# Embedding gather plus position add: streams and semaphores written by hand, and chunks of two sequences instead of one

## The chip, the cores and the metric

The kernel runs on one core of one Trainium2 chip. The metric is device microseconds of that core; lower is better. The kernel before has a median of 184.83 us over 4 runs (184.72 to 184.98).

## The reference

For each of 32 sequences of 512 indices a row of 512 float32 numbers (2 KB) is taken out of a table of 50000 rows, and the row of the position is added. Nothing is reused but the position rows, so 32 MiB (33.55 MB) are read from the table and 32 MiB are written.

```python
def reference(indices, embedding_table, position_embed):
    # indices (32, 512), table (50000, 512) f32, position_embed (512, 512) f32
    token_embed = embedding_table[indices]
    return (token_embed + position_embed).astype(np.float32)
```

## The kernel before

A sequence b is laid out over 128 partitions with K = 4 consecutive positions in each, so partition p holds positions 4p to 4p+3. The position rows are loaded once (line 56, four DMAs of 256 KB), copied by ScalarE to PSUM (line 79, `pos_ps0` to `pos_ps3`), and stay there. The indices come twice: those of sequence 0 straight into the layout that a gather wants (`idx0`, line 49), and all of them in rows (`idx_raw`, line 51), which VectorE turns to float (line 68), TensorE transposes (line 73) and VectorE turns back to int32 (`idx_t`, line 75).

Then the loop over b runs. For each k of 0 to 3 GpSimd (POOL) issues one indirect DMA (line 88) that gathers 128 rows of 2 KB, 256 KB in all, into `data[:, j, :]`; VectorE (DVE) adds `pos_ps[k]` in place (line 94); and after the n parts of a chunk SyncE (SP) issues the store (line 97). A chunk is a whole sequence for most b: one store of 1 MB in which each partition writes 4 rows that lie together, 8 KB. The first two sequences and the last one are cut into four stores of 256 KB with 2 KB for each partition, the four after the start and the last but one into two of 512 KB with 4 KB. There are 128 gathers, 128 adds and 46 stores.

The order is not written out by hand: the tile framework orders the instructions, gives each DMA one of eight semaphores for gathers and one of eight for plain transfers, and inserts the waits. So a gather waits for the gather eight before it, a store for the store eight before it, and a gather into a used buffer (a pool of 20 buffers of 8 KB for each partition) for that buffer's store as well. A wait that doesn't fit onto an instruction is an instruction of its own ahead of it on the same engine. At the end SP waits for all these semaphores, two for each waiting instruction, before the engines meet in a closing barrier. Each engine works through its instructions in order. Gathers and stores go through different queues to the same 16 DMA engines.

Of the kernel before, what the change touches and what calls it, by code (L numbers as in the profile page):

```python
# [1 line left out]

# [4 lines left out]

P = 128
K = 4
BUFS = 20  # L10


@with_exitstack
def kernel(
    ctx: ExitStack,
    tc: tile.TileContext,
    indices: bass.AP,
    embedding_table: bass.AP,
    position_embed: bass.AP,
    out: bass.AP,  # L20
):

    nc = tc.nc
    f32 = mybir.dt.float32
    i32 = mybir.dt.int32
    add = mybir.AluOpType.add

    B, S = indices.shape
    V, D = embedding_table.shape
    assert S == P * K and B == 32  # L30
    assert V < (1 << 24), "an index passes through float32"


    idx_words = indices.bitcast(i32)
    idx_first = idx_words[0].rearrange("(p w) -> p w", p=P)
    out_rows = out.rearrange("b (p k) d -> b p k d", k=K)
    pos_rows = position_embed.rearrange("(p k) d -> p k d", k=K)
    table = embedding_table[:, :]

    const = ctx.enter_context(tc.tile_pool(name="const", bufs=1))  # L40
    data_pool = ctx.enter_context(tc.tile_pool(name="data", bufs=BUFS))
    psum = ctx.enter_context(
        tc.tile_pool(name="psum", bufs=1, space=bass.MemoryType.PSUM)
    )

    idx0 = const.tile([P, 2 * K], i32)
    nc.sync.dma_start(out=idx0[:], in_=idx_first)
    idx_raw = const.tile([B, S, 2], i32)  # L50
    nc.sync.dma_start(
        out=idx_raw[:], in_=idx_words.rearrange("b (s w) -> b s w", w=2)
    )
    pos_sb = [const.tile([P, D], f32, name=f"pos_sb{k}") for k in range(K)]
    for k in range(K):
        nc.sync.dma_start(out=pos_sb[k][:], in_=pos_rows[:, k, :])


    ones = const.tile([B, B], f32)
    nc.gpsimd.memset(ones[:], 1.0)  # L60
    ident = const.tile([B, B], f32)
    nc.gpsimd.affine_select(  # L62
        out=ident[:], in_=ones[:], pattern=[[-1, B]],
        compare_op=mybir.AluOpType.is_equal, fill=0.0, base=0,
        channel_multiplier=1,
    )
    idx_f = const.tile([B, P, K], f32)
    nc.vector.tensor_copy(  # L68
        out=idx_f[:].rearrange("b p k -> b (p k)"), in_=idx_raw[:, :, 0]
    )  # L70
    turned = psum.tile([P, K, B], f32)
    for k in range(K):
        nc.tensor.transpose(turned[:, k, :], idx_f[:, :, k], ident[:])  # L73
    idx_t = const.tile([P, K, B], i32)
    nc.vector.tensor_copy(out=idx_t[:], in_=turned[:])  # L75

    pos_ps = [psum.tile([P, D], f32, name=f"pos_ps{k}") for k in range(K)]
    for k in range(K):
        nc.scalar.copy(out=pos_ps[k][:], in_=pos_sb[k][:])  # L79

    def chunk(b, parts):
        at = 0
        for n in parts:
            data = data_pool.tile([P, n, D], f32, tag="data")
            for j in range(n):
                k = at + j
                where = idx0[:, 2 * k : 2 * k + 1] if b == 0 else idx_t[:, k, b : b + 1]
                nc.gpsimd.indirect_dma_start(  # L88
                    out=data[:, j, :],
                    out_offset=None,  # L90
                    in_=table,
                    in_offset=bass.IndirectOffsetOnAxis(ap=where, axis=0),
                )
                nc.vector.tensor_tensor(  # L94
                    out=data[:, j, :], in0=data[:, j, :], in1=pos_ps[k][:], op=add
                )
            nc.sync.dma_start(out=out_rows[b][:, at : at + n, :], in_=data[:])  # L97
            at += n

    for b in range(B):  # L100
        if b <= 1 or b == B - 1:
            chunk(b, (1, 1, 1, 1))
        elif b <= 5 or b == B - 2:
            chunk(b, (2, 2))
        else:
            chunk(b, (K,))


# [1 line left out]
_INS = ['indices', 'embedding_table', 'position_embed']  # L110
_OUTS = [((32, 512, 512), 'float32')]


# [23 lines left out]
```

## Time and profile before

| what | value |
|---|---|
| median of 4 runs | 184.83 us |
| the profiled execution's own time | 184.92 us |
| span from its first to its last instruction | 183.2 us, so 1.7 us lie around it |
| POOL, 128 gathers of about 0.945 us | 121 us busy, from 2.8 to 163.4 us |
| DVE, 128 adds of 0.687 us | 87 us busy |
| ACT, PE | 3.6 us and 0.7 us busy, all at the start |
| moved by DMA | 68.33 MB, 373 GB/s over the span |

The busy time of POOL is the time in which it makes the descriptors of a gather, not the transfer; the transfers are in the DMA rows. In the rows by slices each digit or number is one fortieth of the span, 4.58 us. A store or load shows on SP (as SPq) only with the time of its issue.

### The profile page before, as it was taken

To read this page: it belongs to the slowest core of one execution; us is meant where nothing else is said; L and a number is where in the kernel's file an instruction comes from. 1 tells how busy PE (TensorE), PEld (TensorE's weight loads), DVE (VectorE), ACT (ScalarE), POOL (GpSimd) and SP (SyncE) were. 2 spreads that over 40 slices of the span, in tenths; PEclk is the share of its full clock that TensorE was granted. 3 is DMA by queue.
4 is the path that set the end of the run, shared out by engine and by line. 5 is a ranking of instruction groups with operands and counts; after the bars stand their busy time and mean duration, and the time that the engine had idled before them with its cause. 6 is when DMAs were issued, how large, how long until landed. Compare 5 with 4: busy or idle time off the path is not lost.

```text
span 183.2 us, 480 instructions
## 1 busy us (share of the span) xinstructions
PE 0.7 (0%) x4; PEld 0.6 (0%) x4; DVE 87.7 (48%) x130; ACT 3.6 (2%) x5; POOL 121.7 (66%) x134
## 2 busy tenths in 40 slices
PE   0000000000000000000000000000000000000000
PEld 0000000000000000000000000000000000000000
DVE  1253553645545444555555464454547464644400
ACT  2500000000000000000000000000000000000000
POOL 4777777777777777777777777777877677750000
DMA  4989999999999999999999999999999999999900
GB/s 133 311 285 361 364 382 380 396 391 409 402 399 388 425 404 405 400 411 419 422 411 413 418 414 413 412 412 418 415 420 412 416 411 424 406 424 409 369 12 0
DMA packets 17635, 68.33 MB, mean 373 GB/s; under 512 B 3008, under 2 KB 3008, under 8 KB 14560
## 3 DMA queue, kind: packets, MB, share of 16 engines
q0 software_dynamic: 10240, 33.56, 48.2%
q1 hardware_dynamic: 7392, 34.74, 46.3%
q14 instruction: 3, 0.02, 0.0%
HBM read 34.74 MB, written 33.55 MB: 373 GB/s over the span
## 4 chain that ended last, share of the span: by engine, by line
issue 43%; DMA 27%; POOL 14%; SPq 5%; POOLq 3%; DVE 1%
DMA data<-in_embedding_table_dram,idx_t 20%; POOL data L88 14%; DMA out_dram<-data 6%; SPq L97 5%; POOLq L88 3%; DVE data L94 1%; DMA idx<-in_indices_dram 1%
## 5 line engine op out<-in xcount | busy, mean ns | idle before, releaser
L88 POOL DMA_INDIRECT data<-in_embedding_table_dram,idx_t x124 | 117.2, 945 | 38.6 <-issue 37.4
L94 DVE TENSOR_TENSOR data<-data,pos_ps 128x512 f32<-128x512 f32 x128 | 86.8, 687 | 80.5 <-issue 54.0
L88 POOL DMA_INDIRECT data<-in_embedding_table_dram,idx x4 | 4.0, 993 | 2.5 <-DMA idx<-in_indices_dram 1.6
L79 ACT COPY pos_ps<-pos_sb 128x512 f32<-128x512 f32 x4 | 2.4, 589 | 4.5 <-DMA pos_sb<-in_position_embed_dram 3.7
L68 DVE CAST idx_f<-idx_raw 32x512 f32<-32x512 int32 x1 | 0.6, 639 | 3.5 <-DMA idx_raw<-in_indices_dram 3.5
L79 ACT ACT_TABLE_LOAD x1 | 1.3, 1283 | 0.8 <-PEq L121 0.8
L75 DVE CAST idx_t<-turned 128x128 int32<-128x128 f32 x1 | 0.3, 291 | 0.8 <-PE turned L73 0.8
L73 PE MATMUL turned<-ident,idx_f 32*128 32x32 f32 x4 | 0.7, 300 | 4.3 <-DVE idx_f L68 4.3
L73 PEld LDWEIGHTS turned<-ident,idx_f 32*128 32x128 f32 x4 | 0.6, 206 | 4.3 <-issue 4.3
L121 POOL MEMSET const-float32-0.0<- 128x1 f32 x1 | 0.1, 104 | 0.3 <-issue 0.3
L60 POOL MEMSET ones<- 32x32 f32 x1 | 0.1, 114 | 0.3 <-POOLq L121 0.3
L62 POOL TENSOR_SCALAR_AFFINE_SELECT ident<-ones 32x32 f32<-32x32 f32 x1 | 0.2, 203 | 0.1
L121 POOL MEMSET const-uint8-127<- 128x1 uint8 x1 | 0.1, 121 | 0.0
L121 POOL MEMSET const-bfloat16-1.0<- 128x1 bf16 x1 | 0.1, 115 | 0.0
L121 POOL MEMSET const-float32-1.0<- 128x1 f32 x1 | 0.1, 107 | 0.0
## 6 DMA issues: line engine op xcount, KB each, us to landing
out_dram<-data SPq DMA_DIRECT2D x24, 1024.0 KB
out_dram<-data SPq DMA_DIRECT2D x10, 512.0 KB
out_dram<-data SPq DMA_DIRECT2D x12, 256.0 KB
data<-in_embedding_table_dram,idx_t POOLq DMA_INDIRECT x124
pos_sb<-in_position_embed_dram SPq DMA_DIRECT2D x4, 256.0 KB
idx_raw<-in_indices_dram SPq DMA_DIRECT2D x1, 128.0 KB
data<-in_embedding_table_dram,idx POOLq DMA_INDIRECT x4
idx<-in_indices_dram SPq DMA_DIRECT2D x1, 4.0 KB
```

The lines of the kernel that those rows point to most:

```text
L60: nc.gpsimd.memset(ones[:], 1.0)
L62: nc.gpsimd.affine_select(out=ident[:], in_=ones[:], pattern=[[-1, B]], compare_op=mybir.AluOpType.is_equal, fill=0.0, base=0, channel_mul ...
L68: nc.vector.tensor_copy(out=idx_f[:].rearrange("b p k -> b (p k)"), in_=idx_raw[:, :, 0])
L73: nc.tensor.transpose(turned[:, k, :], idx_f[:, :, k], ident[:])
L75: nc.vector.tensor_copy(out=idx_t[:], in_=turned[:])
L79: nc.scalar.copy(out=pos_ps[k][:], in_=pos_sb[k][:])
L88: nc.gpsimd.indirect_dma_start(out=data[:, j, :], out_offset=None, in_=table, in_offset=bass.IndirectOffsetOnAxis(ap=where, axis=0),)
L94: nc.vector.tensor_tensor(out=data[:, j, :], in0=data[:, j, :], in1=pos_ps[k][:], op=add)
L97: nc.sync.dma_start(out=out_rows[b][:, at : at + n, :], in_=data[:])
L121: nc = _bacc.Bacc("TRN2", target_bir_lowering=False, num_devices=1)
```

## The change

Everything after the tiles are made is put into one critical section, within which the framework orders nothing and sets no waits: five streams of instructions, one for each engine, with semaphores by hand. Each gather, add and store carries its waits itself. Sixteen semaphores take turns for the gathers, so a gather waits for the one sixteen before it; a store's semaphore is waited for only where its slot is used again, and the last ones share one semaphore, on which SP waits once at the end.

The chunk becomes two sequences: K = 8, so each partition holds 8 consecutive positions, 16 KB; partitions 0 to 63 belong to the first sequence of the pair and 64 to 127 to the second. There are 16 units of 8 gathers of 256 KB, 11 slots of 16 KB for each partition, and 22 stores: most of them are 2 MB with 16 KB for each partition; unit 0 is stored in parts of 2, 2 and 4 gathers, unit 1 in 4 and 4, the last unit in 4, 2, 1 and 1.

As both halves of the partitions need the same position rows, the table of positions is loaded once (four DMAs of 256 KB, two issued by SP and two by ScalarE) and copied twice into PSUM: 16 copies of 64 partitions instead of 4 of 128. It fills all of PSUM, so the transposed indices are put in the last eighth of it, and the copies of the last position wait until they have been read. There are 8 small transposes instead of 4. The load of all indices moves from second to last on SP's queue, behind the position loads that SP issues.

```diff
-K = 4
-BUFS = 20
+K = 8
+H = P // 2
+SLOTS = 11
+LANES = 16
...
+    stores = []
+    for u in range(U):
+        parts = {0: (2, 2, 4), 1: (4, 4), U - 1: (4, 2, 1, 1)}.get(u, (K,))
...
+    def load_pos(engine, k):
+        half, at = divmod(k, K // 2)
+        engine.dma_start(
+            out=pos_sb[half * H : (half + 1) * H, at : at + 2, :],
+            in_=pos_rows[:, k : k + 2, :],
+        ).then_inc(s_pos[k // 2], 16)
+
+    with tc.tile_critical(no_gpsimd_drain=True):
+
+
+        nc.sync.dma_start(out=idx0[:], in_=idx_first).then_inc(s_first, 16)
+        load_pos(nc.sync, 0)
+        load_pos(nc.scalar, 4)
+        load_pos(nc.sync, 2)
+        load_pos(nc.scalar, 6)
+        nc.sync.dma_start(
+            out=idx_raw[:], in_=idx_words.rearrange("u (s w) -> u s w", w=2)
+        ).then_inc(s_raw, 16)
...
+        nc.gpsimd.wait_ge(s_first, 16)
+        for g in range(U * K):
+            u, k = divmod(g, K)
+            if g == K:
+                nc.gpsimd.wait_ge(s_idx, 1)
+            if u >= SLOTS and k == 0:
+                done = sum(1 for x in stores if x[0] == u - SLOTS)
+                nc.gpsimd.wait_ge(s_out[u - SLOTS], 16 * done)
+            where = idx0[:, 2 * k : 2 * k + 1] if u == 0 else idx_t[:, k, u : u + 1]
+            ins = nc.gpsimd.indirect_dma_start(
+                out=slots[u % SLOTS][:, k, :],
...
+            ).then_inc(s_gather[g % LANES], 16)
+            if g >= LANES:
+                ins._wait_ge(s_gather[g % LANES], rounds(g - LANES))
...
+        for g in range(U * K):
+            u, k = divmod(g, K)
+            if u == 0:
+                nc.vector.wait_ge(s_ps, 2 * (k + 1))
+            part = slots[u % SLOTS][:, k, :]
+            nc.vector.tensor_tensor(
+                out=part, in0=part, in1=pos_ps[:, k, :], op=add
+            )._wait_ge(s_gather[g % LANES], rounds(g)).then_inc(s_add, 1)
+
+
+        for k in range(K):
+            half, at = divmod(k, K // 2)
+            if k % 2 == 0:
+                nc.scalar.wait_ge(s_pos[k // 2], 16)
+            if k == K - 1:
+                nc.scalar.wait_ge(s_idx, 1)
+            for to in range(2):
+                nc.scalar.copy(
...
+        for u, at, n in stores:
+            done = s_out.get(u, s_rest)
+            rest += done is s_rest
+            nc.sync.dma_start(
+                out=out_rows[u][:, at : at + n, :],
+                in_=slots[u % SLOTS][:, at : at + n, :],
+            )._wait_ge(s_add, u * K + at + n).then_inc(done, 16)
+        nc.sync.wait_ge(s_rest, 16 * rest)
```

## The prediction

> **What bounds the kernel now.** I read the page's slices first, then groups, waits, stretches, last the end of the timeline.
>
> ```profile
> POOL 4777777777777777777777777777877677750000
> DMA  4989999999999999999999999999999999999900
> ...
> q0 software_dynamic: 10240, 33.56, 48.2%
> q1 hardware_dynamic: 7392, 34.74, 46.3%
> ...
> L88 POOL DMA_INDIRECT data<-in_embedding_table_dram,idx_t x124 | 117.2, 945 | 38.6 <-issue 37.4
> L94 DVE TENSOR_TENSOR data<-data,pos_ps 128x512 f32<-128x512 f32 x128 | 86.8, 687 | 80.5 <-issue 54.0
> ```
>
> DMA is full from the second slice to the 38th, and 48.2 + 46.3% of 183.2 us is 173 us of transfer on every engine. POOL looks only 7 tenths busy, but its idle time is "issue": between two gathers lie 0.30 us that nothing releases. It works at its own pace, 0.945 + 0.30 = 1.25 us a gather.
>
> ```profile
> POOL data L88 <- issue: 38.3, 123, 0.7
> ...
> POOL data L88 <- DMA data<-in_embedding_table_dram,idx_t: 1.2, 4, 0.3
> ```
>
> In the whole run it waits 1.2 us for transfers. From 2.81 to 163.45 us it issues 128 gathers: a floor.
>
> ```profile
> 10.00:20.00 10.00, 0.00 (x0) 0.00 (x0) 4.75 (x7) 0.00 (x0) 7.56 (x9) 1.00 0.97 324
> 20.00:40.00 20.00, 0.00 (x0) 0.00 (x0) 10.17 (x15) 0.00 (x0) 15.12 (x17) 1.00 1.03 391
> ...
> 120.00:140.00 20.00, 0.00 (x0) 0.00 (x0) 10.76 (x17) 0.00 (x0) 14.94 (x17) 1.00 1.02 415
> ...
> 175.00:184.00 9.00, 0.00 (x0) 0.00 (x0) 0.00 (x0) 0.00 (x0) 0.00 (x0) 1.00 0.00 0
> ```
>
> The last two columns are DMA share and GB/s. A gather (0.262 MB) and its store each 1.25 us want 419 GB/s; DMA gives 415. So two limits lie within 1% of each other. And in the last 9 us nothing runs at all.
>
> ```profile
> 171.84 3.51 SPq L97 DMA_DIRECT2D out_dram<-data  x2
> 171.90 0.69 DVE L94 TENSOR_TENSOR data<-data,pos_ps 128x512 f32<-128x512 f32 x1 [0.54 <-DMA out_dram<-data]
> ```
>
> The page doesn't count semaphore instructions; the trace's records have them. The last store packet ends at 174.6. SP then goes through ten instructions that wait for semaphores, at 176.04, 177.43, 178.15, 178.84, 179.54, 180.24, 180.94, 181.65, 182.34 and 182.34: most are 0.70 apart, though the same kind took 0.017 in mid-run. From 182.34 the closing barrier takes 0.85.
>
> **What the Trainium skill says.** "DMA: Bandwidth & Descriptors", section "Queues, rings and completion order": each engine goes round between the queues that have work, one packet at a time. The trace agrees: an engine has 8 packets of a 1 MB store, 8 x (311 + 163.5 ns, below) = 3.8 us if one gather packet stands between each two, and the store issued at 160.76 ran from 163.74 to 167.79, 4.05. Same page, "Why small descriptors are slow": each packet carries a fixed cost. Packet records, median ns for one engine:
>
> ```
> 2 KB store 84 (1536 of them)   4 KB store 159   8 KB store 309 (mean 311)
> 4 KB gather 159, mean 163.5 from 60 us on; 214 beside 2 KB stores (10 to 20 us)
> semaphore write 9
> ```
>
> That is 9 ns and 75 for every 2 KB. "Perfetto Trace Analysis", "Identifying Dependency Chains": waits that don't fit stand as instructions ahead; SP's list here shows one before nearly every store.
>
> **The change, part by part.** My sum follows the end: last gather, its add, its store, SP's closing.
>
> *Entry.* A hand-over from SP to all engines, one semaphore each way: barrier instructions in this trace are 0.04 to 0.1 us apart; I take 0.2 (0.1 to 0.5). It moves POOL's first gather, so everything.
>
> *Positions, indices.* 12 more ACT copies are 12 x 0.589 = 7.1 us, 4 more transposes about 0.5, a cast twice as long 0.6. Two loads issued from ACT (about 0.43 each, as on SP) push its table load (1.28) to 3.1 us, still before the first position rows at 4.73. Position k is then ready at 4.7 + 1.2(k+1), the last at 14.3. `idx_raw` goes behind two position loads on SP's queue and shares with ACT's two: 1 MB took until about 8 us before, so I let it land at 7.3 instead of 3.5. Cast 1.2, transposes 1.2, cast 0.3: `idx_t` at 10.0. POOL needs it for gather 8 at 3.0 + 8 x 1.25 = 13.0, so 3 us of cover. If that is gone, all 120 remaining gathers stand behind this wait and each us of lateness is a us at the end. The first add, behind both casts on DVE, moves from 8.2 to about 10. Taken: 0.
>
> *Semaphores in the middle.* The lanes of eight cost POOL 1.2 us at most; sixteen allow a lag of 20 us, so this can go. The five slot waits look at stores issued some 90 us earlier: 0. The instructions taken from DVE and SP were off the path there. Range -1.2 to 0, taken: 0, since a POOL that is earlier meets full DMA.
>
> *Packets of 16 KB.* By the line above 9 + 8 x 75 = 609 ns (an estimate; not seen here; if it is cut in two, 618). Per engine and pair of sequences: before 32 gather packets x 163.5 + 16 store packets x 311 + 10 x 9 = 5.23 + 4.98 + 0.09 = 10.30 us; the stretches show 1.02 for full, so 10.10 of wall against POOL's 10.00. After: 5.23 + 8 x 609 = 4.87, + 0.08 = 10.18, or 9.98. DMA goes from 1% too slow to just even. What it lost has been a growing lag: from end of issue to add, 4.5 to 6.8 us around 45 us, 6.7 to 8.5 near the end, so 2 us. Gain at most 2.
>
> *Stores twice as large.* A 2 MB store stands on the engines for 8 x (609 + 163.5) = 6.2 us. In that time 5 gathers, 20 packets for each engine, arrive and 8 are served; 12 x 0.16 = 2 us of lag are added at its end. I follow the end of the run with a base lag of 4 us: gather 119 is issued by 153.6, its add done at 158.3, the store starts 2.7 later (as the 8 KB stores do) and runs from 161 to 167.2. Gathers 124 to 127 wait behind it, share the engines with the 1 MB part until 171, and the last lands at 171.5. So the gain of 2 is given back: last add 171.9 to 172.6 and last store packet at 174.6, as before. With 0.2 of entry, 174.8. From both sides: 172 where the lag at the end stays near 5 us, 179 where gather packets take 170 ns beside 16 KB ones (the rival below).
>
> *Fewer stores early.* Unit 2's store leaves at about 37.5, where before there was one every 2 us. Between 27.5 and 37.5 the engines have 1 MB of stores (2.5) and 8 gathers (5.1), so 2.4 us idle. They cost nothing while POOL sets the pace; they count if DMA does.
>
> *Closing.* After the last packet, 0.4 to the semaphore. Then one wait for `s_rest` and about seven instructions on SP, four with waits, instead of ten waits: if as fast as mid-run 0.3, at 0.70 each 4.9. Both slow stretches of SP in this trace (36.9 to 40.2 and from 170.4) come after the small-packet stores; the change has half as many 2 KB packets at the end and no waiting instructions between the stores. That speaks for the fast side without showing it; I take 1.3. Barrier 0.85.
>
> Sum: 174.8 + 0.4 + 1.3 + 0.85 = 177.35 of span, against 183.2. Around it lie 184.92 - 183.2 = 1.7: 179.0 us. The profiled execution is 0.09 above the median, which I leave.
>
> **Rivals.** *The closing stays slow.* SP's 0.70 for each instruction is not tied to their number. Then 4.9 instead of 1.3, up to the old 7.7: 182.6 to 185. For it: it began before the final waits, on ordinary stores.
>
> *DMA gets better than even.* Gathers beside small stores took 214 and 187 ns early; that disappears, the lag at the end is 5 us: last add at 168.7, last packet about 171, and a fast closing: 171.2 + 0.4 + 0.3 + 0.85 + 1.7 = 174.5; with my 1.3, 175.5. Against it: the last 2 MB store.
>
> *Slower: large packets starve the gathers.* Place: 16 KB store packets beside gathers from unit 2 on. If a gather packet takes 170 ns or more beside them instead of 163.5, a pair needs 10.4 us, 0.4 over POOL's pace, and 13 such units lose 5 us: last packet at 179.8. With a closing of 0.4 + 1.3 + 0.85 that is 184.1, with the slow one (4.9) 187.7. It decides from about 170 ns with a slow closing, 171 with mine. For it: early gathers beside stores at 174 to 187 ns. Against it: the packets got faster, not slower, as the stores grew (163.5 beside 8 KB).
>
> That the change doesn't do what it says is excluded: the built program has the 16 KB stores and one wait on SP at its end.
>
> **How the numbers follow.** Likeliest (last packet 174 to 175.5, short closing, 177.5 to 181): 0.50. Slow closing: 0.20, 0.04 of it within 0.2% of before and 0.01 slower. Better DMA: 0.17. Slower: 0.13, 0.01 of it at no change. Faster by over 0.2% (what a measurement here can tell) 0.82, same 0.05, slower 0.13. Range 175.5 to 184.6: left out are about 0.05 below and 0.14 above.
>
> **What would show it.** Right: no row of waits on SP after the last store; POOL at 1.25 us a gather; stretches from 40 us at about 419 GB/s; last add near 172. Packets of 16 KB near 609 ns and gathers at 160 to 165 settle the fourth part. Wrong: a gap on POOL before gather 8, lags over 9 us, gather packets over 170 ns, or SP still at 0.70 for each instruction after the last packet.

## The result, and the profile after

The kernel after takes 185.02 us (median of 32 runs, 184.56 to 185.3), the kernel before beside it 184.78 (52 runs, 184.6 to 185.12). The ratio is 1.0012, interval 1.0007 to 1.0017: 0.24 us slower, where 5.8 us faster was forecast. The profiled execution of after took 184.94 us with a span of 183.2, that of before 184.92 with 183.2. In two of the five groups of experiments the kernel before itself takes 178.2 to 178.5 us instead of 184.5, because a stretch of slow waits at the end of SP, described below, is missing there; so each ratio belongs to the runs of its own group.

The page of after: slices, DMA queues, groups.

```profile
POOL 3777777777777777777777777777777778750000
DMA  5999999999999999999999999999999999999960
...
q0 software_dynamic: 10240, 33.56, 49.2%
q1 hardware_dynamic: 3504, 34.22, 45.5%
q10 hardware_dynamic: 160, 0.52, 1.1%
...
L128 POOL DMA_INDIRECT slot<-in_embedding_table_dram,idx_t x120 | 113.5, 946 | 36.6 <-issue 36.6
L157 DVE TENSOR_TENSOR slot<-slot,pos_ps 128x512 f32<-128x512 f32 x128 | 85.8, 687 | 77.8 <-DMA slot<-in_embedding_table_dram,idx_t 51.5
```

POOL is as before: 946 ns a gather, and idle time that is only "issue". DMA is not: its row goes on into the 39th slice, where before it ended with the 38th. The packets of stores and loads fell from 7392 to 3664 (q10 has the loads that ScalarE issues), but their share of the engines did not fall with them: 46.6% for 46.3%. The share of the gathers rose from 48.2 to 49.2%. And DVE, whose idle time was mostly "issue" before, now waits for gathers.

The waits of after (total, times, longest, in us):

```profile
DVE slot L157 <- DMA slot<-in_embedding_table_dram,idx_t: 51.5, 25, 4.3
POOL slot L128 <- issue: 38.7, 127, 0.3
...
DVE idx_f L146 <- DMA idx_raw<-in_indices_dram: 9.1, 1, 9.1
...
POOL slot L128 <- DMA idx<-in_indices_dram: 1.8, 1, 1.8
```

POOL waits once, for the first indices, and never for a gather, a slot or `idx_t`. DVE's 51.5 us come in 25 waits of up to 4.3 us: the gathers arrive in bunches.

The windows of after; the last columns are DMA share and GB/s:

```profile
20.00:40.00 20.00, 0.00 (x0) 0.00 (x0) 11.19 (x17) 0.00 (x0) 15.13 (x17) 1.00 0.99 374
40.00:60.00 20.00, 0.00 (x0) 0.00 (x0) 8.77 (x14) 0.00 (x0) 15.13 (x17) 1.00 0.99 379
...
120.00:140.00 20.00, 0.00 (x0) 0.00 (x0) 10.85 (x16) 0.00 (x0) 15.12 (x17) 1.00 1.02 413
...
175.00:184.00 9.00, 0.00 (x0) 0.00 (x0) 0.00 (x0) 0.00 (x0) 0.00 (x0) 1.00 0.22 88
```

Before, these four were 391, 398, 415 and 0 GB/s; the second of them:

```profile
40.00:60.00 20.00, 0.00 (x0) 0.00 (x0) 11.35 (x17) 0.00 (x0) 15.12 (x17) 1.00 1.01 398
```

From 20 to 60 us the kernel after moves (17 + 19) GB/s x 20 us = 0.72 MB less, which is 1.7 us of full DMA, and what is missing there is still under way after 175 us. The rest is 0.31 MB in the first 20 us (187 and 331 GB/s against 225 and 324, in windows of 10 us) and 0.3 MB between 80 and 160 us, 0.7 us each: about 3.2 us in all. The DMA share of after is 0.99 between 20 and 60 us, against 1.02 later, so at most 1.2 of the 40 us are idle there; for the rest the engines move less while they are busy.

The end of after in the timeline (start, length, engine, line, operation, idle before):

```profile
171.60 0.69 DVE L157 TENSOR_TENSOR slot<-slot,pos_ps 128x512 f32<-128x512 f32 x1 [3.00 <-issue]
172.32 2.80 SPq L179 DMA_DIRECT2D out_dram<-slot  x2
174.07 0.69 DVE L157 TENSOR_TENSOR slot<-slot,pos_ps 128x512 f32<-128x512 f32 x1 [1.78 <-DMA slot<-in_embedding_table_dram,idx_t]
```

The last add starts 2.17 us later than before (171.90). What follows it stands only in the trace's records:

```
after:  last store packet ends 177.94; SP passes the wait for s_rest at 178.35
        SP   178.61 drain    178.79 wait, 0.70 long   180.89 wait, 1.40 long   182.30 through
        POOL 178.63 drain, 2.515 long (ends 181.15);  closing barrier to 183.19
before: last store packet ends 174.60; SP's ten waits stand at 176.04 ... 182.34
        POOL 160.56 drain, 12.21 long (ends 172.77);  closing barrier to 183.16
```

DMA ends 3.34 us later, and yet SP is through at the same time in both kernels: 182.34 before, 182.30 after. By steps, in us:

| | before | forecast | after | after in the fourth group, without the stretch |
|---|---|---|---|---|
| last gather issued | 163.45 | | 163.24 | 162.95 |
| last store packet ends | 174.60 | 174.8 | 177.94 | 177.30 |
| SP past the wait for the last stores | | 175.2 | 178.35 | 177.72 |
| closing barrier can begin | 182.34 | 176.5 | 182.30 | 180.52 |
| span | 183.2 | 177.35 | 183.2 | 181.4 |

### The profile page after: what moved, and what is told of

Same layout as the page of the kernel before. It is cut to its first block, busy times and chain, and to the rows that moved or that the text cites. A ratio compares the mean times of both kernels' runs of the same rounds, so it can differ in the third digit from the quotient of the medians.

```text
span 183.2 us, 395 instructions
## 1 busy us (share of the span) xinstructions
PE 1.1 (1%) x8; PEld 1.0 (1%) x8; DVE 86.7 (47%) x130; ACT 10.6 (6%) x17; POOL 121.9 (67%) x134
## 3 DMA queue, kind: packets, MB, share of 16 engines
q0 software_dynamic: 10240, 33.56, 49.2%
## 4 chain that ended last, share of the span: by engine, by line
POOL 65%; issue 22%; DMA 7%; DVE 0%; SPq 0%; POOLq 0%
POOL slot L128 65%; DMA slot<-in_embedding_table_dram,idx_t 6%; DMA idx<-in_indices_dram 1%; DVE slot L157 0%; SPq L209 0%; POOLq L126 0%; SPq L100 0%
## 5 line engine op out<-in xcount | busy, mean ns | idle before, releaser
L128 POOL DMA_INDIRECT slot<-in_embedding_table_dram,idx_t x120 | 113.5, 946 | 36.6 <-issue 36.6
L157 DVE TENSOR_TENSOR slot<-slot,pos_ps 128x512 f32<-128x512 f32 x128 | 85.8, 687 | 77.8 <-DMA slot<-in_embedding_table_dram,idx_t 51.5
L128 POOL DMA_INDIRECT slot<-in_embedding_table_dram,idx x8 | 7.8, 980 | 3.9 <-issue 2.1
L169 ACT COPY pos_ps<-pos_sb 64x512 f32<-64x512 f32 x16 | 9.3, 584 | 3.1 <-DMA pos_sb<-in_position_embed_dram 2.8
L146 DVE CAST idx_f<-idx_raw 16x1024 f32<-16x1024 int32 x1 | 0.7, 727 | 9.1 <-DMA idx_raw<-in_indices_dram 9.1
L140 PE MATMUL pos_ps<-ident,idx_f 16*128 16x16 f32 x8 | 1.1, 268 | 9.9 <-DVE idx_f L146 9.9
L140 PEld LDWEIGHTS pos_ps<-ident,idx_f 16*128 16x128 f32 x8 | 1.0, 198 | 9.9 <-DVE idx_f L146 9.9
```

The source lines that it names most:

```text
L128: ins = nc.gpsimd.indirect_dma_start(out=slots[u % SLOTS][:, k, :], out_offset=None, in_=table, in_offset=bass.IndirectOffsetOnAxis(ap=whe ...
L140: ins = nc.tensor.transpose(turned[:, k, :], idx_f[:, :, k], ident[:])
L146: nc.vector.tensor_copy(out=idx_f[:].rearrange("u p k -> u (p k)"), in_=idx_raw[:, :, 0])._wait_ge(s_raw, 16).then_inc(s_cast, 1)
L157: nc.vector.tensor_tensor(out=part, in0=part, in1=pos_ps[:, k, :], op=add)._wait_ge(s_gather[g % LANES], rounds(g)).then_inc(s_add, 1)
L169: nc.scalar.copy(out=pos_ps[to * H : (to + 1) * H, k, :], in_=pos_sb[half * H : (half + 1) * H, at, :],).then_inc(s_ps, 1)
```

## The experiments

Two things needed a cause: that DMA ends 3 us later than forecast, and that SP is held until 182.3. The theory for the first: DMA sets the pace, and coarse stores come late and leave it short of work at the start. Its rivals: large packets slow the gathers by themselves; POOL's pace sets the end anyway; the order of the first loads. For the second: a price of each instruction, a price of each DMA packet, POOL's drain, or a time that simply passes. Diffs are against the kernel after.

### First group: the parts of the change, and the stores (before beside it: 178.24 us)

The streams by hand with the old chunk and the old cuts of the stores:

```diff
-K = 8
...
-SLOTS = 11
+K = 4
+SLOTS = 24
...
-        parts = {0: (2, 2, 4), 1: (4, 4), U - 1: (4, 2, 1, 1)}.get(u, (K,))
+        if u <= 1 or u == U - 1:
+            parts = (1, 1, 1, 1)
+        elif u <= 5 or u == U - 2:
+            parts = (2, 2)
+        else:
+            parts = (K,)
...
```

(the position rows are then loaded as before, in four parts of 128 partitions, but two of them are still issued by ScalarE; each is copied once)

> The hand-written streams alone, with the old chunks (K = 4, 24 slots of 8 KB, stores cut as in the kernel before). Theory A (two effects cancel: the streams shorten what SP does after the last packet by 3.4 us, the larger chunks make the last packet 3.3 us late): last packet near 174.6 us as before, 5.2 us after it as in the changed kernel, span 179.8, about 181.5 us, ratio 0.982. Theory B (something else ends both kernels near 182.3 us of the span, whatever the streams and chunks do): 184.8 us, ratio 1.000.

Measured: 182.01 us, ratio 1.0212 (1.0185 to 1.0239), so the streams alone cost 3.8 us here. The time is near that of theory A, but not the ratio of 0.982: the kernel before itself takes 6.5 us less here than in the result. The last store packet ends at 176.11. The first gather is issued at 4.38 us instead of 2.81, and POOL's wait for its indices shows why; here it is in before and in this kernel:

```profile
POOL data L88 <- DMA idx<-in_indices_dram: 1.6, 1, 1.6
...
POOL slot L131 <- DMA idx<-in_indices_dram: 3.0, 1, 3.0
```

The packets of that small load lie at 2.36 to 3.63 us, before at 1.80 to 2.20, and those of the loads that ScalarE issues begin at 2.00, ahead of it. In after it is the other way round: the indices begin at 2.04, ScalarE's loads at 2.31. At the end SP's waits take 0.028 us each, and POOL's drain stands there alone, 2.515 us from 176.80 on. This was the first sight of an end without the stretch.

The chunk of two sequences in the framework's own order:

```diff
-K = 4
-BUFS = 20
+K = 8
...
+BUFS = 11
...
```

(against the kernel before, with the doubled position copies and the store cuts of after)

> The larger chunks alone: the framework's order and waits, K = 8, 11 buffers of 16 KB, stores cut as in the changed kernel. Theory A: last packet near 177.9 us, and the long closing of the kernel before (8.6 us after it): span 186.5, about 188.2 us, ratio 1.018. Theory B: 184.8 to 185 us.

Measured: 181.16 us, ratio 1.0153 (1.0109 to 1.0196): the chunk alone costs about 2.9 us, roughly, as its six runs spread from 180.24 to 183.32. Both theories had expected 184.8 us or more. Its trace is not used here.

The stores of after in halves, 8 KB for each partition:

```diff
-        parts = {0: (2, 2, 4), 1: (4, 4), U - 1: (4, 2, 1, 1)}.get(u, (K,))
+        parts = {0: (2, 2, 4), 1: (4, 4), U - 1: (4, 2, 1, 1)}.get(u, (4, 4))
```

> The changed kernel with every 2 MB store issued as two of 1 MB (units of 8 gathers, packets of 8 KB, each store after its four adds). Theory A says that long stretches with gathers alone cost (170 ns for a packet of 4 KB against 159 beside a store): they shorten from about 4 us in 10 to 1 in 5, so gather packets fall to 164 ns, lag at the end to about 8 us, last packet to 175 to 175.5, span 180.5, about 182.2 us, ratio 0.986. Theory B: 185 us.

Measured: 181.69 us, ratio 1.0182 (1.0148 to 1.0216); last store packet at 175.76, gather packets 163.9 ns. Its windows:

```profile
20.00:40.00 20.00, 0.00 (x0) 0.00 (x0) 10.49 (x16) 0.00 (x0) 15.12 (x17) 1.00 1.00 388
40.00:60.00 20.00, 0.00 (x0) 0.00 (x0) 10.20 (x16) 0.00 (x0) 15.13 (x17) 1.00 1.01 394
```

Against the profile of after in the result that is 14 and 15 GB/s more, 0.58 MB or 1.4 us, of the 2.2 us by which the last packet is earlier. Against that of after in the fourth group, which has no stretch either (390 and 375 GB/s, last packet at 177.30), it is 0.34 MB or 0.8 us, of 1.5. The sign is the same; the size differs from one profile of after to the next.

The stores of units 1 to 14 left out:

```diff
+            if u not in (0, U - 1):
+                continue
```

(POOL's waits for a free slot then look at the adds, as there is no store to wait for)

> The changed kernel without the stores of units 1 to 14 (that part of the output is not written): the pace of the gathers alone. POOL is the limit: last gather issued by 163.3, landed by 167, last packet by 169, then 5.2 us of closing as in the changed kernel: span about 174, 176 us by theory A. If gathers without stores take 170 ns for a packet, the lag stays under 4 us all the same, since 64 packets on 16 engines are then 0.68 us of each 1.25. Theory B (a fixed end): span still about 183.

Measured: 176.88 us, ratio 0.9925 (0.9896 to 0.9954).

```profile
60.00:80.00 20.00, 0.00 (x0) 0.00 (x0) 11.01 (x17) 0.00 (x0) 15.13 (x17) 1.00 0.73 210
```

With half the traffic DMA is 0.73 busy, an add follows the end of its gather's issue by 2.8 us, and the last packet ends at 171.10. POOL's pace alone would thus end the transfers at about 171. After ends them at 177 to 178: those 6 to 7 us are DMA's, so DMA and not POOL sets the end.

### Second group: POOL's drain and the first load (before: 184.54 us, with the stretch)

Before and after once more, unchanged:

> The kernel before itself, for a trace from the chip on which its variants run. In the runs beside the first experiments it took 178.24 us, not 184.8. Theory C: the ten waiting instructions of SP at the end then take 0.06 us each as in the variants of those runs, so SP is through 0.6 us after the last store has landed; last packet near 174.6 as before, span about 176.5. If instead the transfers are faster on that chip, the last packet is near 168 and SP's waits are still 0.70 apart.

> The changed kernel itself beside the kernel before on the same chip. Theory C (three terms: the last packet 3.3 us later; POOL's drain of 2.5 us, which now stands behind the last store; ten waits fewer on SP, worth 6 us only where SP is slow at its end): with a quick SP last packet 177.9, closing 0.45 + 0.25 + 2.5 + 0.75, span 182, about 183.7 us and a ratio near 1.031; with a slow SP 185 us and 1.001. Theory B (a fixed end): a ratio of 1.00 on this chip too.

Measured: 184.54 us, ratio 1.0 (0.9992 to 1.0009), and 184.85, 1.0015 (1.0008 to 1.0022). The stretch is there: SP's waits in before are 0.70 us, or a multiple of it, apart from 172.3 us to 182.08, and in after two waits last from 178.03 to 182.11.

A drain of POOL right after the last gather:

```diff
                 ins._wait_ge(s_gather[g % LANES], rounds(g - LANES))
+        nc.gpsimd.drain()
```

> The changed kernel with one drain more on POOL, behind its last gather, where it runs beside the last transfers. If the drain of 2.5 us at the end is work left over from the gathers, it shrinks to about 0.1 us there, and the kernel is 2.3 us shorter than the changed one (181.4 us where that takes 183.7). If a drain costs 2.5 us whenever it comes, there is no difference. Where SP is slow at its end, at most 0.5 us either way, since SP is the last to arrive there.

Measured: 184.85 us, ratio 1.0016 (1.0008 to 1.0024), the same as after. But the drain at the end shrank from 2.515 to 0.041 us: its work was done beside the transfers. SP, through at 182.28, held the end. The drain is a cost only where the stretch is missing. There it should give back about 2.2 us (its end at 180.52 against SP's at 178.34 in the fourth group); that is worked out, and was not run by itself.

The same drain with `K = 4`, and the load of all indices second on SP's queue again (against the first kernel of the first group):

```diff
         nc.sync.dma_start(out=idx0[:], in_=idx_first).then_inc(s_first, 16)
+        nc.sync.dma_start(
+            out=idx_raw[:], in_=idx_words.rearrange("u (s w) -> u s w", w=2)
+        ).then_inc(s_raw, 16)
         load_pos(nc.sync, 0)
         load_pos(nc.scalar, 1)
...
+        nc.gpsimd.drain()
```

> The streams by hand with the old chunks, with the early drain, and with the load of all indices second on SP's queue as in the kernel before. Theory C: last packet near 175.0 (174.6 and 0.4 of entry), no drain left, so span 175.0 + 0.45 + 0.3 + 0.75 = 176.5, 178.2 us: ratio 1.00 with a quick SP, 0.98 with a slow one. A rival: the drain isn't what costs, then 180.5.

Measured: 186.19 us, ratio 1.0085 (1.007 to 1.0099), a miss. The first gather went to 5.19 us, and SP is through only at 184.41, 2.3 us later than in after.

```profile
POOL slot L131 <- DMA idx<-in_indices_dram: 3.8, 1, 3.8
```

The packets of the first load now lie at 2.35 to 4.08 us. The place of `idx_raw` doesn't cure its delay; what still differs from before is that ScalarE issues loads at the same time.

### Third group: what the stretch is, and all loads from SP (before: 184.55 us, with the stretch)

Five more adds on DVE behind the last store, for which the end must wait (they change a slot that has been stored already):

```diff
+        nc.vector.wait_ge(s_rest, 16 * sum(1 for x in stores if x[0] >= U - SLOTS))
+        for k in range(5):
+            ins = nc.vector.tensor_tensor(out=last, in0=last, in1=pos_ps[:, k, :], op=add)
```

> The changed kernel with five adds more on DVE that wait for the last stores (about 3.5 us of work in the closing; the extra adds write only a slot that has been stored). Two readings of SP's slow closing: if it is a stretch of time that passes anyway after the last packet (4.4 to 4.8 us in the changed kernel), the adds hide under it and the time grows by 0.5 us at most. If each of SP's last instructions costs 0.70 after whatever it waits for, the time grows by about 3.5 us. Where SP is quick at its end, POOL's drain of 2.5 us hides most of the adds: 0.6 to 1.2 us more.

Measured: 184.94 us, against 184.91 of after in this group. The end of its timeline:

```profile
172.27 2.74 SPq L187 DMA_DIRECT2D out_dram<-slot  x3
177.82 3.57 DVE L164 TENSOR_TENSOR slot<-slot,pos_ps 128x512 f32<-128x512 f32 x5 [4.27 <-DMA out_dram<-slot]
```

3.57 us of new work at the very end cost nothing. SP's two waits, let go at 181.47 when DVE was done, took 0.028 us each. So the stretch is not a price that these instructions pay once their wait is over: a time passes, and work beside it is free. A delay that an instruction takes while it waits anyway would look the same here; against a price for each instruction speaks that ten waits in before and two in after end at the same time.

`K = 4` once more, with every load from SP in the order of before, and the early drain (against the last kernel of the second group):

```diff
-        load_pos(nc.scalar, 1)
+        load_pos(nc.sync, 1)
         load_pos(nc.sync, 2)
-        load_pos(nc.scalar, 3)
+        load_pos(nc.sync, 3)
```

> Streams by hand, old chunks, early drain, and all loads at the start issued by SP in the order of the kernel before. Theory: loads of positions that ScalarE issues at the same moment overtake the first 4 KB of indices on the DMA engines, which put off the first gather to 4.4 and 5.2 us in the two hand-written kernels with old chunks (2.8 before). Then it is at 2.9 to 3.0 here, the last packet at 174.6 to 174.8, and the time 178 us where SP is quick (ratio 1.00), 184.5 where it is slow. If it is something else, the first gather stays over 4 us.

Measured: 184.09 us, ratio 0.9969 (0.9959 to 0.998), below both kernels. The first gather is back at 2.88 us, the first add at 8.02.

```profile
POOL slot L131 <- DMA idx<-in_indices_dram: 1.5, 1, 1.5
```

Only the issuer of two loads has changed, and 2.3 us of wait are gone. The last store packet ends at 174.61, as in before (174.60), and SP is quick again at 182.2. This version was not run without the stretch.

The halves with the same two cures, and after again:

```diff
-        parts = {0: (2, 2, 4), 1: (4, 4), U - 1: (4, 2, 1, 1)}.get(u, (K,))
+        parts = {0: (2, 2, 4), 1: (4, 4), U - 1: (4, 2, 1, 1)}.get(u, (4, 4))
...
-        load_pos(nc.sync, 0)
-        load_pos(nc.scalar, 4)
-        load_pos(nc.sync, 2)
-        load_pos(nc.scalar, 6)
...
+        for k in range(0, K, 2):
+            load_pos(nc.sync, k)
...
+        nc.gpsimd.drain()
```

> The changed kernel with stores of 1 MB (two for each unit), the loads at the start as in the kernel before, and the early drain: all three suspected costs taken away. Last packet 177.4 less 1.7 (stores) less 0.5 to 1 (start): 174.7 to 175.2. With a quick SP 175 + 0.45 + 0.3 + 0.75 + 1.7 = 178.2 us, ratio 1.00; with a slow one, whose stretch after the last packet lies between 4.8 us (13.9 thousand packets) and 7.7 (17.6 thousand), 15.8 thousand give about 6.2: 183.4 us, ratio 0.994.

> The changed kernel beside the other three on whatever chip they get. With a quick SP: last packet 177.4 to 177.9, closing 0.45 + 0.25 + 2.5 + 0.75, so 183.2 to 183.7 us and a ratio near 1.03; with a slow one 184.9 us and 1.001 as before.

Measured: 184.27 us, ratio 0.9986 (0.9979 to 0.9992), last packet at 175.68; for after 184.91, 1.0018 (1.0011 to 1.0026), last packet at 178.15. A DMA end that is 2.5 us earlier makes 0.6 us of time: the stretch takes the rest.

### Fourth group: the size of the stores (before: 178.52 us, without the stretch)

Every gather stored by itself, 128 stores of 256 KB with packets of 2 KB, beside after:

```diff
-        parts = {0: (2, 2, 4), 1: (4, 4), U - 1: (4, 2, 1, 1)}.get(u, (K,))
+        parts = (1,) * K
```

> The changed kernel with every gather stored by itself: 128 stores of 256 KB with packets of 2 KB, some 29 thousand packets in all instead of 13.9. The engines then need 16384 x 84 ns / 16 = 86 us for stores instead of 78, and gathers beside such stores took up to 214 ns: last packet at 188 to 196. If the length of the slow stretch goes with the number of packets (0.8 us for a thousand, from 4.6 at 13.9 and 7.7 at 17.6 thousand), 15 us or more follow it: over 206 us. If both kernels ended at 182.3 for another reason, the stretch has passed by then: last packet, 3.9 us of closing and 1.7, so 194 to 202 us.

> The changed kernel beside the other three. In a session with the slow stretch 184.9 us, ratio 1.002. In one without it (the kernel before at 178.2): last packet 177.3 to 178.1, then 0.7 to the join, 2.5 of POOL's drain and 0.75: 183.0 to 183.9 us, ratio 1.03.

Measured: 180.77 us, ratio 1.0128 (1.0107 to 1.0149), and for after 183.49, 1.0297 (1.0261 to 1.0334). One edit moves the last packet from 177.30 to 174.88 us, where 188 to 196 was expected: the small packets did not make the transfers slow. The windows of after in this group:

```profile
20.00:40.00 20.00, 0.00 (x0) 0.00 (x0) 11.66 (x18) 0.00 (x0) 15.12 (x17) 1.00 1.01 390
40.00:60.00 20.00, 0.00 (x0) 0.00 (x0) 8.26 (x14) 0.00 (x0) 15.13 (x17) 1.00 1.00 375
60.00:80.00 20.00, 0.00 (x0) 0.00 (x0) 11.36 (x17) 0.00 (x0) 15.12 (x17) 1.00 1.02 413
```

and those of the kernel with single stores:

```profile
20.00:40.00 20.00, 0.00 (x0) 0.00 (x0) 10.61 (x17) 0.00 (x0) 15.13 (x17) 1.00 1.03 402
40.00:60.00 20.00, 0.00 (x0) 0.00 (x0) 11.35 (x17) 0.00 (x0) 15.12 (x17) 1.00 1.04 410
60.00:80.00 20.00, 0.00 (x0) 0.00 (x0) 11.21 (x17) 0.00 (x0) 15.13 (x17) 1.00 1.04 412
```

From 60 us on both move the same, 413 and 412 GB/s, one with packets of 16 KB and the other of 2 KB. The difference lies between 20 and 60 us: (12 + 35) GB/s x 20 us = 0.94 MB, 2.3 us at 412 GB/s, against a DMA end that is 2.42 us earlier. So once the stores flow, the size of their packets makes no difference, and what the fine stores gain lies before. There the engines of after are hardly idle: their share is 1.01 and 1.00, against 1.02 later, which leaves 0.6 us of the 2.3. The rest is packets that took longer: between 20 and 60 us a packet of a 16 KB store took 708 ns on the mean (614 from 70 us on) and a gather packet 173, against 162 with single stores. The edit makes the stores earlier and their packets smaller at once, and it cuts the first two units and the last one finer too; which of these does it was not separated.

The kernel with few stores again, and twelve late adds instead of five:

> The changed kernel without the stores of units 1 to 14 once more (that part of the output is not written); in a session in which SP was quick it took 176.88 us with its last packet at 171.1. In a session with the slow stretch: if the stretch goes with the packets (11.8 thousand), 2.8 us of it hide under POOL's drain, and it takes 177 us again. If the end is fixed near 182.3, it takes 184.8 us.

> The changed kernel with twelve adds more on DVE behind the last stores, 8.7 us of work instead of 3.6 (they write only a slot that has been stored). If the slow stretch is time that passes, the first 4 us are free and the rest is paid: DVE done at 186.8, 1.1 us more for the join and barrier, 189.5 us. If SP's last instructions cost 0.70 each whenever they come, 192 us or more.

Measured: 177.11 us, ratio 0.9912 (0.9888 to 0.9935), last packet at 171.41, as in the first group; and 190.24, 1.0675 (1.0625 to 1.0725). Without the stretch late work does cost (twelve adds; five were not run without it). DVE is done at 186.94, 6.4 us after the end of POOL's drain in after (180.52), and the time grows by 6.75. SP's waits take 0.028 us.

### Fifth group: many packets (before: 184.53 us, with the stretch)

Single stores with all loads from SP and the early drain, once with `K = 4` and once with `K = 8` (shown for `K = 8`):

```diff
+        parts = (1,) * K
...
+            load_pos(nc.sync, k)
...
+        nc.gpsimd.drain()
```

> Streams by hand, old chunks (K = 4), each gather stored by itself, loads at the start all from SP in the old order, early drain. The stores start at 9 us instead of 12.5 and are never in a burst, so gather packets stay at 159 ns: last packet 173.5 to 174.3 (174.9 in the kernel with chunks of two and such stores, 174.6 in the one with the old stores). Closing 0.45 + 0.3 + 0.75. Without the slow stretch 176.7 to 177.5 us, ratio 0.99 to 0.995 of the kernel before. With the stretch: 184 us as for the old stores if it ends at a fixed time, over 190 us if it goes with the number of packets (29 thousand).

> The same with units of 8 gathers: adds start about 2.5 us later than in the kernel with old chunks, as all positions are copied twice and the indices are turned later. Last packet 174.3 to 174.9; without the slow stretch 177.5 to 178.1 us, ratio 0.995 to 1.0; with it the same two readings as above.

Measured: 185.25 and 185.27 us, both 1.0039 (1.0026 to 1.0053). SP's issues from 160 us on, in the first of them:

```profile
160.55 21.00 SPq L172 DMA_DIRECT2D out_dram<-slot  x16
```

and in the kernel with single stores of the fourth group, without the stretch:

```profile
159.98 9.17 SPq L179 DMA_DIRECT2D out_dram<-slot  x8
```

With the stretch SP needs 21.00 us for 16 stores, some 1.4 us each, and falls behind: the last add starts at 167.97, the last store packet ends at 180.41. Its records are spaced like this from 64 us on. At 182.25 (182.62 with `K = 8`) it is quick again. These two kernels have some 29 thousand packets and after has 13.9 thousand, and the stretch ends at about the same time: a price of each packet would have moved it.

## Why the prediction was wrong

The span was forecast 5.85 us too short. Two terms of the sum failed: 3.14 us at the last packet and 2.65 in the closing, and both would have had to hold for the forecast time.

*Closing* (1.3 us) is the step that decided the measured time. It took 3.95 us (178.35 to 182.30). The forecast read SP's 0.70 us as a price of instructions, of which there would be fewer. The runs show a time until which SP is slow: 182.34 in before with ten waits, 182.30 in after with two; work put beside it is free. With `K = 4` and all loads from SP the last packet was at 174.61, better than the forecast's 174.8, and the time still 184.09. This was the first rival, "The closing stays slow", 182.6 to 185, and its reason, "not tied to their number", was right; 0.20 was too small a chance for it. Its sum was another, though: from a last packet at 174.8 it needed 7.3 us of closing to reach 185. The packet came 3.1 us later and the closing was 3.95, and only because the end is a date do the two make up for each other; that the time lies at the edge of this rival is partly luck. The 0.24 us by which after is slower are of the size of its later first gather (0.37 us in the profiles of the result, 0.12 in the second group's); the closing barrier too is longer, 0.94 us for 0.87. That these are their cause is argued, not shown.

One part of the closing was not named at all: POOL's drain of 2.515 us. In before it stood beside the last transfers; in after it comes behind the wait for the last store. It is hidden in the stretch where there is one, and sets the end where there is none: 178.00 + 2.515 = 180.52 us in the fourth group.

*Fewer stores early* (0: "They cost nothing while POOL sets the pace; they count if DMA does") is the term behind most of the late DMA. DMA does set the pace: with few stores the transfers end 6 to 7 us earlier and POOL is unchanged. Bytes that are missing early are moved at the end, since later windows run at their 408 to 413 GB/s anyway. Measured: 0.7 us in the first 20 and 1.7 between 20 and 60; single stores won back 2.4. The loss did not take the form that the forecast saw, 2.4 us of idle engines between 27.5 and 37.5 us: by the share, 0.99 for 1.02, at most 1.2 us are idle between 20 and 60, and 0.6 in the fourth group. The rest is longer packets there: 662 ns for 16 KB (708 in the fourth group) and 179 for a gather (173), where later they took 614 and 168. Why they are longer just there stays open.

*Packets of 16 KB*: the 609 ns were right (median 611, mean 614 from 70 us on), the gain was not there. Gather packets went from 163.9 ns (163.5 in the forecast) to 167.7, the mean from 60 us on, so a pair of sequences takes 32 x 167.7 + 8 x 614 + 80 ns = 10.36 us, 10.16 of wall, against 10.10 before and 9.98 forecast. The third rival had large packets starve the gathers, and they don't: from 70 us on gather packets of after take 160 ns while half or more of the engines have a 16 KB store packet and 171 where none has, and coarse stores leave more time of that kind. With single stores they took 159.1 from 60 us on. The Trainium skill, "DMA: Bandwidth & Descriptors", section "Rules for kernel authors", asks for 1 MiB or more in each DMA for the highest bandwidth; here stores of 256 KB and of 2 MB both gave 412 to 413 GB/s once they flowed, and the small ones were done sooner.

*Stores twice as large* was right in kind and 2 us short: the lag from the end of a gather's issue to its add grew from 8.1 us (gather 64) to 10.8 (the last gather), where before has 8.5 at most. The last gather landed at 173.25, not 171.5, and the last add started at 174.07, not 171.9.

*Positions, indices* (0): right for POOL, which had no gap before gather 8. The first add came at 11.19 us, not at about 10. The loads issued from ScalarE were counted only for ScalarE's own queue; with `K = 4`, where their packets come first, they also delay the first indices, by 1.4 us. In after, where the indices come first, the wait is 1.8 us for 1.6, and 1.5 in its other profiles. The skill, same page, "Issuing engines are not separate DMA queues", says that DMAs of all issuers interleave on the same 16 engines; the packets of the index load at 2.36 to 3.63 us instead of 1.80 to 2.20 agree.

*Entry* (0.2) measured 0.37 in this trace and 0.12 in the second group's. *Semaphores in the middle* (0) was right: POOL waits for nothing but its own pace.

What stays open is the stretch itself. It is there in three of the five groups and in the measurement of the result, and absent in two, for the same kernels. It does not belong to a chip: the first and the third group ran on one chip, the fourth and the fifth on another, each once without it and once with it. In all traces with it but one SP is quick again 179.1 to 179.6 us after the first gather: 2.81 and 182.34 in before, 3.18 and 182.30 in after, 5.19 and 184.41 where the first gather was late. That is 128 x 1.40 us, and there are 128 gathers; but their number was never varied, so a link between them is a guess. The one is the kernel with five late adds, where SP was quick already at 181.47, 178.4 us after the first gather; a fixed end alone doesn't explain that.

## What to carry to other kernels

Where DMA is the bound, compare the bytes moved in each window from the first microsecond on, and not only the busy share: here the engines were 99 to 101% busy while they moved up to 9% less, and no later window gave that back. Finer stores did away with the loss. Before a row of slow waits at the end is priced by their number, put harmless work beside it: if the time doesn't grow, it is a date and not a price. Where an order is taken over by hand, look for what the old order had hidden, here a drain of 2.5 us and a first load that had its queue to itself.

## What the runs showed of the hardware

- SP's records lie 0.70 us or a multiple of it apart, where the same waits take 0.028 otherwise, until about 179 us after the first of 128 gathers (178.4 at most in one trace); present in some groups of runs only, on two chips both with and without (before: 184.5 against 178.2 to 178.5 us).
- A drain of POOL behind its gathers takes 2.515 us when it first runs after they have landed, 0.041 when another has run earlier.
- From 70 us on a gather packet of 4 KB takes 160 ns beside stores and, at moments without one, 171 in after (16 KB stores) and 167 in before and in the kernel with halves (8 KB). With hardly any stores in the run, and the engines 0.73 busy, its median is 159 and its mean 225. Store packets take 84, 159, 309 and 611 ns (medians) for 2, 4, 8 and 16 KB.
- The small load of the first indices lands 1.4 us later (3.63 for 2.20) where the packets of loads of 256 KB that ScalarE issues begin ahead of its own (2.00 and 2.36 us, `K = 4`); in after, where they begin behind it (2.31 and 2.04), it lands at 2.56, in after's later profiles at 2.27 to 2.35.
